# A 4-layer hybrid decoder step on one core: adaLN units placed elsewhere around the pooling layers and two hand-overs

## Chip, cores and metric

The kernel runs on one core of one Trainium2 chip. The metric is the device time of one execution in microseconds, here the median of several runs.

## What is computed

One inference step of a decoder trunk of four layers, with the same weights for a prompt of 256 tokens and for 8 samples of 4 tokens each. D_MODEL is 1024, D_FF 2816. Cut to what matters:

```python
for i in range(DEPTH):                       # 4 layers
    kind, j = i % 3, i // 3
    mod = (silu(c) @ w_ada[i] + b_ada[i])    # six vectors of 1024 for each sequence
    shift1, scale1, gate1, shift2, scale2, gate2 = mod
    h = rms_norm(x, norm_gain[i, 0]) * (1 + scale1) + shift1
    if kind == 0: mix, st = pool_mixer(h, pool_past[j], pos0, pool_w[j], pool_scale[j])
    elif kind == 1: mix, bufs = dilated_attention_mixer(h, ...)
    else: mix, st = gla_mixer(h, gla_past[j], ...)
    x = x + gate1 * mix
    h = rms_norm(x, norm_gain[i, 1]) * (1 + scale2) + shift2
    f, st = conv_ffn(h, conv_past[i], ffn_w_in[i], ffn_conv_w[i], ffn_conv_b[i], ffn_w_down[i])
    x = x + gate2 * f
y = rms_norm(x, final_gain)
```

Layers 0 and 3 pool, layer 1 is dilated attention, layer 2 is GLA (gated linear attention). A pooling layer also returns the samples' last 15 rows of pooling input, 11 of which are copied from the old state.

## The kernel before

All of x stays in SBUF, transposed (features on partitions), as `x` of 8 tiles of 128 features by 288 tokens (256 of the prompt, 32 of the samples). Weights come in units of 1 MB through six `raw` buffers, loaded by SyncE's queue. A product in full precision is made of three: a weight tile is split into a high part `whi` (ScalarE, line 345) and a low part `wlo` (VectorE, line 353), the activations into `hh` and `hl`, and TensorE adds hh*whi, hl*whi and hh*wlo (lines 414 to 416).

The adaLN vectors (`mod`) of a layer come from w_ada, 24 units of 1 MB. A *unit* here is one such load and its matmuls on the `adaps` tile in PSUM (line 534, four column tiles side by side, a moving operand of 512 columns). Units stand in groups; a group gives one or two of the six vectors. `adaps` has one buffer, so a group's end has two steps: its evacuation to `adasb` by ScalarE (line 544), and its finish, four transposes on TensorE (`ps<-adasb`, line 410) with VectorE's additions into `modT` and `modA` (lines 555 to 563). `modA` of a layer is what its norms multiply by.

The order of the program is written by hand as lists of step names: `POOL_ORDERS`, `ATTN_ORDER`, `GLA_ORDER`, `FFN_RUNS`. Every engine follows this order in its own queue. A `+` stands for the next unit of the queue of units, whatever it is. In the first layer the units of groups 1 to 3 are named: b10 to b13 are the units of the first of them, b14 its evacuation, b15 its finish, and likewise b20 to b25 and b30 to b35. In `fill` (line 218), the end of a group is put behind its last unit by three pieces of weights for the evacuation and five for the finish, and earlier in two cases: a step with `need` makes what it needs come out, and a unit that is the `first` of its group makes all pending ends come out ahead of it, since it writes `adaps` anew.

Between the mixer and the FFN of a layer, and between layers, lies a *hand-over*: two `+`, then the sums of squares over x on TensorE (`sqps`, line 596), then the norm. The norm is a chain: ScalarE takes the root (`ny`, `nv`, lines 635 and 636), VectorE makes `rstd` of it (lines 638 to 642), multiplies it with x and `modA` (`ht`, line 674), ScalarE adds the shift and rounds (`hh`, line 705) and VectorE takes the rest (`hl`, line 710). In the FFNs of layers 1 and 2 four `+` follow the norm in the order, and cover it on TensorE.

A pooling layer normalizes, multiplies by its weights in two products (`product0`, `product1`, lines 1019 to 1021), then does the samples' part. `dd` (the samples' differences, last made on GpSimd at line 1000) is multiplied in `ys0` and `ys1` (lines 1042 to 1045: matmuls with 64 or 32 moving columns), then `add0` and `add1` (lines 1056 to 1060) apply the pooling matrices to the prompt. `past` (line 959) prepares the old state ahead of the layer and, at its end, issues the copy of the 11 rows, a DMA from DRAM to DRAM on GpSimd's queue (line 975).

Of the kernel before, what the change touches and what calls it, by code (L numbers as in the profile page):

```python
# [41 lines left out]
norm b10 norm2 b11 product0 product1 ys0 b12 b13 b14 ys1 b15 gates b20 b22 b21 add0 squares0 b23 add1 b24 pre b30 squares1 b25 b31 root  # L42
early b32 b33 b34 b35 end
""", """
norm + + + + norm2 gates product0 product1 pre ys0 ys1 add0 squares0 add1 + + squares1 end
# [12 lines left out]
v0a z0 x2 v0b xc ms7 e2 v0c z1 m0a sb v0d sc ms5 m0b v1a x3 z2 m1a v1b e3 ms6 vv0 m1b + v1c x4 z3 m2a v1d e4 ks m2b +  # L58
v2a x5 z4 m3a v2b ps e5 vv1 m3b + v2c x6 z5 m4a v2d e6 up0 m4b + v3a kk0 z6 m5a v3b uo0 vv2 m5b + v3c ea m6a un0a v3d eb m6b un0b +
r0a ec m7a un0c up1 r0b vv3 m7b un0d kk1 gs0 + r0c cr uo1 r0d up2 un1a + r1a kr0 un1b r1b kr1 un1c op0 r1c un1d op1 kk2 gs1 r1d uo2 op2 up3  # L60
# [120 lines left out]
class Step:  # L181


    __slots__ = ("fn", "piece", "unit", "gap", "busy", "ahead", "key", "need", "first")
# [33 lines left out]
def fill(entries, queue):  # L218

    out, ends = [], []  # L220
    queue = list(queue)
    seen = 0

    def take():
        s = queue.pop(0)
        if s.first:
            while ends:
                out.append(ends.pop(0)[1])
        out.append(s)
        k = 3  # L230
        while queue and queue[0].busy:
            ends.append((seen + k, queue.pop(0)))
            k += 2
    for e in entries:
        if e == "+":
            if queue:
                take()
            continue
        if e.need is not None:
            while any(q.key <= e.need for q in queue):  # L240
                take()
            while any(q.key <= e.need for _, q in ends):
                out.append(ends.pop(0)[1])
        out.append(e)
        if e.piece is not None:
            seen += 1
            while ends and ends[0][0] <= seen:
                out.append(ends.pop(0)[1])
    if queue or ends:
        raise ValueError("units left")  # L250
    return out


class Trunk:
# [258 lines left out]
    def ada_steps(self, l, m0, nm, own=None):  # L513
# [53 lines left out]
        for k, s in enumerate(st):  # L567
            s.key, s.first = (l, m0), k == 0
# [356 lines left out]
    def pool_steps(self, l):  # L925
# [33 lines left out]
        def past(v):  # L959
# [15 lines left out]
            nc.gpsimd.dma_start(out=O["pool_s"][j, :, 0:11, :], in_=I["state_pool"][j, :, 4:15, :])  # L975
# [987 lines left out]
    def build(self):  # L1963
# [22 lines left out]
        for n, l in enumerate(Ls):  # L1986
            kind = l % 3
            after = None
            if kind == 0:
# [10 lines left out]
                after = p.pop("outs2")  # L2000
# [7 lines left out]
            if after:  # L2008
                f.insert(4, after)
# [12 lines left out]
            elif n:  # L2022
                f = ["+", "+", Step(lambda: self.sums()), f[0]] + list("+" * 4) + f[1:]
# [102 lines left out]
```

## Time and profile before

| | |
|---|---|
| median of 3 runs | 1376.65 us (1375.03 to 1380.5) |
| the profiled execution: its time, its span | 1377.05 us, 1375.3 us |
| mean granted clock of TensorE | 0.983 |
| busy: PE, PEld, DVE, ACT, POOL | 1324.9, 1196.7, 853.6, 639.2, 203.4 us |
| adaLN units: matmuls of line 534 on `raw` tiles | 736 records, 93.9 us busy |
| read from HBM, written | 300.21 MB, 19.76 MB |

PE is TensorE's matmuls, PEld its weight loads, DVE VectorE, ACT ScalarE, POOL GpSimd, SP SyncE. Times in rows are microseconds from the start of the span. In a timeline a row has its start, its length, engine, line, operation, the tile written and the tile read, a count, and in brackets how long the engine was idle before it and whose end released it. In windows of time the columns are the busy time of each engine, then the granted clock of TensorE (1.00 is full), the share of the DMA engines' time and GB/s. The trace counts two matmul records where the program has one matmul on 32-bit floats, so a unit is four matmuls in the program and eight in the trace.

### The profile page before, as it was taken

What the parts mean: (1) busy time and instruction counts of PE and PEld (TensorE: products, weight loads), DVE (VectorE), ACT (ScalarE), POOL (GpSimd) and SP (SyncE); (2) the same over time, 40 slices, a digit from 0 to 9 for tenths busy, and PEclk for the clock granted to TensorE, in tenths of its full rate; (3) what the DMA queues carried; (4) which work ended last, traced back from release to release, by engine and by line L of the source; (5) the groups of instructions that cost most, each with busy time, mean ns of one, the idle gap of its engine ahead of it and who ended that gap; (6) DMA issues with size and microseconds to landing.
All of it is one profiled execution on the core that took longest, in us unless ns stands there. A gap on an engine that the chain in (4) does not pass through costs nothing.

```text
span 1375.3 us, 25416 instructions
## 1 busy us (share of the span) xinstructions
PE 1324.9 (96%) x10075; PEld 1196.7 (87%) x10075; DVE 853.6 (62%) x1674; ACT 639.2 (46%) x1154; POOL 203.4 (15%) x492
## 2 busy tenths in 40 slices
PE   5899999999999999999999999999999999999997
PEld 3578899998886798899979887799999977999997
DVE  3576565556445776665566656687765566767654
ACT  3364444435444554444345344465444345555442
POOL 2220001002001112211024522121100022110100
PEclk8899999999999999999999999999999988999999
DMA  9998888559545787995494675885555566454520
GB/s 350 366 317 305 271 297 291 176 175 304 178 156 194 252 274 263 389 342 199 147 306 150 219 259 179 308 252 185 178 153 172 174 248 220 154 184 147 175 85 35
DMA packets 206231, 310.48 MB, mean 226 GB/s; under 512 B 7692, under 2 KB 186742, under 8 KB 196496
## 3 DMA queue, kind: packets, MB, share of 16 engines
q1 hardware_dynamic: 201296, 286.82, 62.4%
q0 software_dynamic: 4352, 21.50, 4.1%
q8 instruction: 79, 1.29, 0.4%
q10 hardware_dynamic: 464, 0.54, 0.1%
q14 instruction: 40, 0.33, 0.1%
HBM read 300.21 MB, written 19.76 MB: 233 GB/s over the span
## 4 chain that ended last, share of the span: by engine, by line
PE 84%; DVE 7%; ACT 3%; DMA 3%; POOL 1%; issue 1%; SPq 0%; DVEq 0%; POOLq 0%; ACTq 0%
PE mm L414 22%; PE mm L416 22%; PE mm L415 22%; PE adaps L534 4%; DMA raw<-w_ada 3%; PE ps L410 2%; DVE hl L710 1%; DVE ht L674 1%; DVE wlo L353 1%; PE mm L796 1%; PE ps L1670 1%; PE sqps L596 1%; PE mm L797 1%; PE mm L798 1%; ACT whi L345 1%
## 5 line engine op out<-in xcount | busy, mean ns | idle before, releaser
L414 PE MATMUL mm<-hh,whi 128*128 128x288 f32 x1720 | 514.6, 299 | 5.9 <-ACT hh L705 4.7
L415 PE MATMUL mm<-hl,whi 128*128 128x288 f32 x1720 | 509.6, 296 | 2.4 <-DVE hl L710 2.3
L416 PE MATMUL mm<-hh,wlo 128*128 128x288 f32 x1720 | 509.0, 296 | 2.0 <-DVE wlo L353 2.0
L353 DVE TENSOR_TENSOR wlo<-raw,whi 128x1024 fp32r<-128x1024 f32 (+2 forms) x335 | 398.7, 1207 | 140.0 <-ACT whi L345 139.7
L345 ACT ACTIVATE whi<-raw 128x1024 fp32r<-128x1024 f32 (+2 forms) x335 | 343.2, 1030 | 283.3 <-PE mm L415 204.7
L414 PEld LDWEIGHTS mm<-hh,whi 128*128 128x128 f32 x1720 | 323.4, 188 | 23.4 <-issue 11.5
L415 PEld LDWEIGHTS mm<-hl,whi 128*128 128x128 f32 x1720 | 323.6, 188 | 5.0 <-POOL hs L678 2.1
L416 PEld LDWEIGHTS mm<-hh,wlo 128*128 128x128 f32 x1720 | 323.4, 188 | 3.1 <-DVE wlo L353 2.7
L414 PE MATMUL mm<-ah,whi 128*128 128x288 f32 x704 | 208.5, 296 | 0.0
L416 PE MATMUL mm<-ah,wlo 128*128 128x288 f32 x704 | 208.0, 295 | 0.0
L415 PE MATMUL mm<-al,whi 128*128 128x288 f32 x704 | 206.9, 294 | 0.0
L415 PEld LDWEIGHTS mm<-al,whi 128*128 128x128 f32 x704 | 132.8, 189 | 0.0
L414 PEld LDWEIGHTS mm<-ah,whi 128*128 128x128 f32 x704 | 132.5, 188 | 0.0
L416 PEld LDWEIGHTS mm<-ah,wlo 128*128 128x128 f32 x704 | 132.3, 188 | 0.0
L853 DVE TENSOR_SCALAR c<-ext,vec 128x304 f32<-128x304 f32 x88 | 38.7, 440 | 120.2 <-ACT ext L850 117.8
L856 DVE SCALAR_TENSOR_TENSOR c<-ext,vec,c 128x304 f32<-128x304 f32 x176 | 94.9, 539 | 6.3
L534 PE MATMUL adaps<-raw,cT 128*32 128x512 f32 x736 | 93.9, 633 | 4.6 <-DMA raw<-w_ada 4.6
L862 POOL COPY convS<-ext 128x2 f32<-128x2 f32 x88 | 16.4, 186 | 458.8 <-ACT ext L849 458.8
L849 ACT ACTIVATE ext<-mm 128x256 f32<-128x256 f32 x88 | 34.0, 387 | 83.7 <-PE mm L416 83.7
L859 ACT ACTIVATE ge<-c 128x304 f32<-128x304 f32 x88 | 40.1, 460 | 57.6 <-DVE c L856 57.4
L872 DVE TENSOR_TENSOR a<-ge,mm 128x256 f32<-128x256 f32 x88 | 36.8, 418 | 43.9 <-PE mm L416 40.3
L534 PEld LDWEIGHTS adaps<-raw,cT 128*32 128x32 f32 x736 | 19.9, 112 | 48.6 <-issue 34.8
(394 smaller groups left out, 1497.6 us busy)
## 6 DMA issues: line engine op xcount, KB each, us to landing
raw<-w_ada SPq DMA_DIRECT2D x92, 1024.0 KB, 7.8
raw<-ffn_w_in SPq DMA_DIRECT2D x80, 1024.0 KB, 5.7
raw<-ffn_w_down SPq DMA_DIRECT2D x32, 1024.0 KB, 5.0
raw<-ffn_w_down SPq DMA_DIRECT2D x16, 768.0 KB, 4.2
raw<-gla_w_in SPq DMA_DIRECT2D x12, 1024.0 KB, 6.4
raw<-ffn_w_in SPq DMA_DIRECT2D x16, 512.0 KB, 5.3
win_s<-cache_win_g POOLq DMA_DIRECT2D x16, 512.0 KB, 7.1
raw<-attn_w_in SPq DMA_DIRECT2D x7, 1024.0 KB, 13.0
```

The costliest lines, as they stand in the source:

```text
L345: self.nc.scalar.activation(out=hv, in_=r, func=AF.Copy)
L353: self.nc.vector.tensor_tensor(out=lv, in0=r, in1=hv.bitcast(F32), op=ALU.subtract)
L410: self.nc.tensor.transpose(out=out, in_=in_, identity=self.ident[0:k, 0:k])
L414: mmul(out=out, lhsT=wh, rhs=xh, start=start, stop=False)
L415: mmul(out=out, lhsT=wh, rhs=xl, start=False, stop=False)
L416: mmul(out=out, lhsT=wl, rhs=xh, start=False, stop=stop)
L534: nc.tensor.matmul(out=ps[32 * q:32 * q + 32, :], lhsT=self.cT[:, k * per + r, :], rhs=v[:, r, j * 512:(j + 1) * 512], start=(k == 0), sto ...
L849: nc.scalar.activation(out=e[:, 2:258], in_=ps[t][:, 0:TP], func=AF.Copy)
L853: nc.vector.tensor_scalar(out=c1, in0=e[:, 0:304], scalar1=w[0], scalar2=self.vcol("ffn_conv_b", l * 22 + f), op0=ALU.mult, op1=ALU.add)
L856: nc.vector.scalar_tensor_tensor(out=c1, in0=e[:, k:k + 304], scalar=w[k], in1=c1, op0=ALU.mult, op1=ALU.add)
L859: nc.scalar.activation(out=ge, in_=c1, func=AF.Gelu)
L872: nc.vector.tensor_tensor(out=a[:, 0:TP], in0=ge[:, 0:TP], in1=ps[t][:, 0:TP], op=ALU.mult)
```

## The change

Four edits of the order; no arithmetic is changed.

1. First layer: b12 moves between `product0` and `product1`, b13 and the evacuation b14 move ahead of `ys0`, b20 ahead of the finish b15, b22 ahead of `gates`.
2. The copy of the 11 rows leaves `past` and becomes a step of its own, put at place 30 of the FFN of the same layer.
3. Two `+` leave the GLA layer, and two are put into the last pooling layer between `product1` and `ys0`.
4. `fill` no longer puts all pending ends ahead of the first unit of a group, only as far as the last evacuation among them; a finish then comes by its count of pieces or by a `need`. A new mark `E`, used in the FFNs of layers 1 and 2, puts a pending evacuation there, ahead of the sums.

```diff
-norm b10 norm2 b11 product0 product1 ys0 b12 b13 b14 ys1 b15 gates b20 b22 b21 add0 squares0 b23 add1 b24 pre b30 squares1 b25 b31 root
+norm b10 norm2 b11 product0 b12 product1 b13 b14 ys0 b20 b15 ys1 b22 gates b21 add0 squares0 b23 add1 b24 pre b30 squares1 b25 b31 root
-norm + + + + norm2 gates product0 product1 pre ys0 ys1 add0 squares0 add1 + + squares1 end
+norm + + + + norm2 gates product0 product1 + + pre ys0 ys1 add0 squares0 add1 + + squares1 end
-v0a z0 x2 v0b xc ms7 e2 v0c z1 m0a sb v0d sc ms5 m0b v1a x3 z2 m1a v1b e3 ms6 vv0 m1b + v1c x4 z3 m2a v1d e4 ks m2b +
+v0a z0 x2 v0b xc ms7 e2 v0c z1 m0a sb v0d sc ms5 m0b v1a x3 z2 m1a v1b e3 ms6 vv0 m1b v1c x4 z3 m2a v1d e4 ks m2b +
-r0a ec m7a un0c up1 r0b vv3 m7b un0d kk1 gs0 + r0c cr uo1 r0d up2 un1a + r1a kr0 un1b r1b kr1 un1c op0 r1c un1d op1 kk2 gs1 r1d uo2 op2 up3
+r0a ec m7a un0c up1 r0b vv3 m7b un0d kk1 gs0 r0c cr uo1 r0d up2 un1a + r1a kr0 un1b r1b kr1 un1c op0 r1c un1d op1 kk2 gs1 r1d uo2 op2 up3
...
         if s.first:
-            while ends:
+            while any(q.evac for _, q in ends):
                 out.append(ends.pop(0)[1])
...
+        if e == "E":
+            if ends and ends[0][1].evac:
+                out.append(ends.pop(0)[1])
+            continue
...
-            s.key, s.first = (l, m0), k == 0
+            s.key, s.first, s.evac = (l, m0), k == 0, k == NF // per
...
-            nc.gpsimd.dma_start(out=O["pool_s"][j, :, 0:11, :], in_=I["state_pool"][j, :, 4:15, :])
+        st["copy"] = Step(lambda: nc.gpsimd.dma_start(out=O["pool_s"][j, :, 0:11, :], in_=I["state_pool"][j, :, 4:15, :]))
...
-                after = p.pop("outs2")
+                after = [p.pop("outs2"), p.pop("copy")]
...
-                f.insert(4, after)
+                f[4:4] = after[:1]
+                f[30:30] = after[1:]
...
-                f = ["+", "+", Step(lambda: self.sums()), f[0]] + list("+" * 4) + f[1:]
+                f = ["+", "+", "E", Step(lambda: self.sums()), f[0]] + list("+" * 4) + f[1:]
```

The changed file's lines are numbered four higher from line 243 on (534 becomes 538). TensorE's order in the first layer, from the end of `product1` (`mm<-whi,hl`, `mm<-wlo,hh`) on. Before:

```order
L1020 MATMUL mm<-whi,hl 128x256
L1021 MATMUL mm<-wlo,hh 128x256
L1043 MATMUL ys<-dd,whi 128x64
L1045 MATMUL ys<-dd,wlo 128x32
L1042 MATMUL ys<-dd,wlo 128x32
```

Now:

```order
L1024 MATMUL mm<-whi,hl 128x256
L1025 MATMUL mm<-wlo,hh 128x256
L538 MATMUL adaps<-raw,cT 32x512 x4
L1047 MATMUL ys<-dd,whi 128x64
L1049 MATMUL ys<-dd,wlo 128x32
L1046 MATMUL ys<-dd,wlo 128x32
```

One unit (b13) now stands between the product and the samples' product; another (b12) stands in the same way between the two products.

TensorE's order at the hand-over from GLA to its FFN: the last product of the mixer, the hand-over, the transposes of the convolution's state (`ps<-cm,raw`) and the first product of the FFN. Before:

```order
L416 MATMUL mm<-hh,wlo 128x288
L534 MATMUL adaps<-raw,cT 32x512 x8
L596 MATMUL sqps<-ssq,ones 128x288
L596 MATMUL sqps<-sq,ones 128x288
L534 MATMUL adaps<-raw,cT 32x512 x8
L410 MATMUL ps<-cm,adasb 128x128 x4
L534 MATMUL adaps<-raw,cT 32x512 x8
L410 MATMUL ps<-cm,raw 128x88 x4
L414 MATMUL mm<-hh,whi 128x288
```

Now:

```order
L420 MATMUL mm<-hh,wlo 128x288
L538 MATMUL adaps<-raw,cT 32x512 x8
L600 MATMUL sqps<-ssq,ones 128x288
L600 MATMUL sqps<-sq,ones 128x288
L538 MATMUL adaps<-raw,cT 32x512 x16
L414 MATMUL ps<-cm,raw 128x88 x4
L418 MATMUL mm<-hh,whi 128x288
```

The finish of a group (`ps<-cm,adasb`) has left the place between the units behind the sums; this finish and another of the mixer's last products now come in the FFN. On ScalarE the evacuation ahead of the norm's root is now that of the group whose last unit stands ahead of the sums; before, it was that of the group whose last unit stands behind them.

TensorE's order at the hand-over from the last pooling layer to the last FFN, from the end of `add1` (`mm<-cb,zl`) on. Before:

```order
L1060 MATMUL mm<-cb,zl 128x128
L410 MATMUL ps<-cm,adasb 128x128 x4
L534 MATMUL adaps<-raw,cT 32x512 x8
L596 MATMUL sqps<-ssq,ones 128x288
L596 MATMUL sqps<-sq,ones 128x288 x4
L534 MATMUL adaps<-raw,cT 32x512 x8
L410 MATMUL ps<-cm,raw 128x88 x4
L414 MATMUL mm<-hh,whi 128x288
```

Now:

```order
L1064 MATMUL mm<-cb,zl 128x128
L538 MATMUL adaps<-raw,cT 32x512 x8
L600 MATMUL sqps<-ssq,ones 128x288
L600 MATMUL sqps<-sq,ones 128x288 x4
L414 MATMUL ps<-cm,adasb 128x128 x4
L538 MATMUL adaps<-raw,cT 32x512 x8
L414 MATMUL ps<-cm,raw 128x88 x4
L418 MATMUL mm<-hh,whi 128x288
```

The finish of the group that holds scale2 and shift2 of the last layer has moved from ahead of the units and the sums to behind both. VectorE's order is the same there: `modT`, `modA` and the samples' product with `modA` stand ahead of the norm's root.

More of the change, by code (lines that the diff above doesn't have):

```diff
@@ L181 @@
 class Step:
-    __slots__ = ("fn", "piece", "unit", "gap", "busy", "ahead", "key", "need", "first")
+    __slots__ = ("fn", "piece", "unit", "gap", "busy", "ahead", "key", "need", "first", "evac")
     def __init__(self, fn, piece=None, unit=None, gap=0, busy=False, ahead=None, need=None):
```

## Prediction

> **What bounds the kernel now.** I read the page first, then the list of who waited for whom, then windows of time with the granted clock, then the timeline at the places that the change touches.
>
> ```profile
> span 1375.3 us, 25416 instructions
> PE 1324.9 (96%) x10075; PEld 1196.7 (87%) x10075; DVE 853.6 (62%) x1674; ACT 639.2 (46%) x1154; POOL 203.4 (15%) x492
> ...
> PE 84%; DVE 7%; ACT 3%; DMA 3%; POOL 1%; issue 1%; SPq 0%; DVEq 0%; POOLq 0%; ACTq 0%
> ```
>
> TensorE is busy for 1324.9 of 1375.3 us, and 84% of the chain that ended last is its own work. The number of its instructions does not change here, so only 50.4 us of idle time, and time at a low clock, can be won. The list of waits (total, times, longest) says where PE stood:
>
> ```profile
> PE mm L414 <- ACT hh L705: 4.7, 3, 1.9
> PE adaps L534 <- DMA raw<-w_ada: 4.6, 4, 2.1
> PE ys L1043 <- POOL dd L1000: 2.2, 2, 1.1
> PE ps L410 <- ACT adasb L544: 2.2, 3, 0.7
> ```
>
> These four kinds are the ones that the change is near: FFN starts that wait for the norm, adaLN units that wait for their weights, the two pooling layers' sample products, and the ends of adaLN groups. The windows add what the waits do not show (the first number behind the PE, PEld, DVE, ACT and POOL columns is PE's granted clock):
>
> ```profile
> core 0: us, PE busy (x) PEld busy (x) DVE busy (x) ACT busy (x) POOL busy (x), PEclk, DMA share, GB/s
> 27.40:44.40 17.00, 13.80 (x60) 5.35 (x60) 5.62 (x15) 3.62 (x6) 2.14 (x6) 0.50 1.03 406
> 44.40:56.10 11.70, 9.40 (x72) 8.01 (x71) 10.49 (x22) 5.76 (x13) 6.11 (x12) 1.00 0.97 388
> 56.10:73.00 16.90, 16.85 (x130) 10.38 (x130) 9.47 (x25) 6.84 (x16) 0.00 (x0) 1.00 0.88 327
> 891.00:894.40 3.40, 1.28 (x11) 0.91 (x8) 2.92 (x7) 1.12 (x4) 2.34 (x5) 0.99 1.09 356
> 894.40:897.80 3.40, 3.40 (x17) 3.40 (x16) 3.40 (x9) 2.22 (x5) 0.66 (x1) 0.50 1.09 348
> 1123.00:1126.50 3.50, 2.40 (x22) 2.19 (x20) 2.61 (x7) 3.02 (x6) 1.18 (x6) 1.00 0.64 205
> 1126.50:1143.50 17.00, 17.00 (x79) 13.69 (x80) 10.21 (x26) 4.93 (x12) 0.00 (x0) 0.50 0.23 69
> ```
>
> Three stretches ran at half clock: the start, 3.4 us behind the GLA hand-over, and 17.0 us in the last pooling layer. 17.0 is five times 3.4, so the clock seems to be set in steps of 3.4 us. PE is fully busy in the last two, so they cost half their length, 1.7 and 8.5 us. Each follows a step in which PE did little.
>
> The profiled execution took 1377.05 us, 1.75 us more than its span, and 0.4 us above the median of 1376.65. I sum against 1377.05. About 0.5%, or 6.9 us, is what a measurement of this kernel can tell from no change.
>
> **The row copy.** It leaves the start, where DMA is full (share 1.03 at 406 GB/s in the window 27.40 to 44.40).
>
> ```profile
> 27.41 0.59 POOL L975 DMA_DIRECT2D pool_s<-state_pool  x1
> 34.79 1.93 PE L534 MATMUL adaps<-raw,cT 128*32 128x512 f32 x8 [1.60 <-DMA raw<-w_ada]
> 37.30 1.94 PE L534 MATMUL adaps<-raw,cT 128*32 128x512 f32 x8 [0.58 <-DMA raw<-w_ada]
> ```
>
> In the list of DMA issues (size of one, us to landing) it is:
>
> ```profile
> pool_s<-state_pool POOLq DMA_DIRECT2D x1, 352.0 KB, 6.7
> ```
>
> The copy runs while PE waits for the last two units of the first group, on which the first norm depends. 352 KB at 406 GB/s is 0.9 us. Bounds: 0, if it only used gaps, and -1.8 if reading and writing both count. I take **-0.9**. In the first layer's FFN it is one POOL issue of 0.59 us ahead of a small copy for the convolution. POOL is 15% busy and covers it, and the transfer lies beside products that no wait for DMA in the list belongs to, so I charge nothing; without that cover it would cost its 0.9 us there. The second layer's copy moves from one FFN to the next: nothing.
>
> **First pooling layer.**
>
> ```profile
> 54.15 0.30 PE L1043 MATMUL ys<-dd,whi 128*128 128x64 f32 x1 [1.09 <-POOL dd L1000]
> 56.05 1.92 PE L534 MATMUL adaps<-raw,cT 128*32 128x512 f32 x16
> ```
>
> PE is idle for 11.70 - 9.40 = 2.3 us from 44.4 to 56.1: 1.09 for dd and 1.2 for hl in the products. Two units cost 1.92 us at 56.05. Now one of them (b12) stands between the two products and one (b13) behind them. b13 fills the wait for dd. b12 delays the second product, whose waits for hl it covers; I put that at 0.7 of the 1.2 us, since most of the rest falls in the first product, ahead of it. The sample product then ends at 56.05 - 1.09 - 0.7 + 1.92 = 56.2 with both units done, where that was 56.05 + 1.92 = 58.0: **-1.8**. Bounds: -1.1 (only the wait for dd is filled) to -1.92. Behind it PE is full (16.85 of 16.90 us), so the gain is kept as far as the next norm, which starts earlier by it. The units' weights come in the same order as before. The group's evacuation stands at the same place of ScalarE's queue.
>
> **GLA layer.** Two units leave it.
>
> ```profile
> 757.76 1.06 PE L534 MATMUL adaps<-raw,cT 128*32 128x512 f32 x8
> 801.55 1.06 PE L534 MATMUL adaps<-raw,cT 128*32 128x512 f32 x8
> ```
>
> Neither has idle time ahead of it, so each is some 1.0 us of PE time: **-1.9** for both. They may have covered VectorE work, which then shows as a wait: bound -0.9.
>
> **GLA to FFN.** Below is this hand-over, then the same one behind attention, which has four units and no group's end in it.
>
> ```profile
> 885.94 1.92 PE L534 MATMUL adaps<-raw,cT 128*32 128x512 f32 x16
> 887.93 0.60 ACT L544 ACTIVATE adasb<-adaps 128x512 f32<-128x512 f32 x1 [3.68 <-PE adaps L534]
> 888.42 0.50 ACT L635 ACTIVATE ny<-sqps,eps 128x288 f32<-128x288 f32 x1
> 888.58 0.66 PE L410 MATMUL ps<-cm,adasb 128*128 128x128 f32 x4 [0.72 <-ACT adasb L544]
> 893.14 0.40 PE L414 MATMUL mm<-hh,whi 128*128 128x288 f32 x1 [1.60 <-ACT hh L705]
> ```
>
> ```profile
> 468.56 3.64 PE L534 MATMUL adaps<-raw,cT 128*32 128x512 f32 x32
> 472.57 0.38 PE L414 MATMUL mm<-hh,whi 128*128 128x288 f32 x1
> 479.87 0.40 PE L414 MATMUL mm<-hh,whi 128*128 128x288 f32 x1 [0.41 <-ACT whi L345]
> 481.13 0.40 PE L416 MATMUL mm<-hh,wlo 128*128 128x288 f32 x1 [0.73 <-DVE wlo L353]
> ```
>
> The sums end at 885.94, but ScalarE cannot start the norm's root (ny) until 888.42: the group's evacuation stands ahead of it in its queue and waits for two more units. In the changed order the group that ends here had its last unit before the sums, so its evacuation runs beside them; the ends' transposes go into the FFN. Then the place is like the one behind attention: the first FFN product 472.57 - 468.56 = 4.0 us behind the sums, where it was 893.14 - 885.94 = 7.2. That is -3.2; the half clock behind it goes, -1.7; the two waits that come behind attention (0.41 and 0.73) appear here, +1.1; the 0.66 us of transposes are paid in the FFN, +0.7. Sum **-3.1**. Bounds: -1.6 (the weights' split is later than I think), -3.8.
>
> **Last pooling layer.** Two units stand ahead of its sample products.
>
> ```profile
> 1124.76 0.30 PE L1043 MATMUL ys<-dd,whi 128*128 128x64 f32 x1 [1.10 <-POOL dd L1000]
> 1130.08 0.56 PE L1056 MATMUL mm<-cb,zh 128*128 128x256 f32 x1
> ```
>
> They fill 1.10 us and cost 1.92: **+0.8**. The half clock began at 1126.5, in the midst of the sample products, whose small matmuls (64 and 32 columns) leave the array nearly empty. With the wait filled, the thin stretch is 3.4 us of these products at full clock instead of 4.5. A step of 3.4 us can still lie mostly on it, but then the drop comes at its end, some 1.7 us of work later, which is one step less at half clock: **-1.7**, with bounds 0 and -8.5.
>
> [...]
>
> **Last hand-over.** The end of the group now stands behind the sums.
>
> ```profile
> 1139.77 0.50 DVE L555 TENSOR_TENSOR modT<-ps,vec 128x36 f32<-128x36 f32 x4 [0.39 <-PE ps L410]
> 1140.64 0.42 DVE L667 TENSOR_TENSOR hs<-x,modA 128x256 f32<-128x256 f32 x1
> 1146.30 1.92 PE L534 MATMUL adaps<-raw,cT 128*32 128x512 f32 x16
> 1146.94 0.53 DVE L638 TENSOR_TENSOR ssq<-ny 128x32 f32<-128x32 f32 x2 [5.88 <-ACT ny L635]
> 1149.81 0.40 PE L414 MATMUL mm<-hh,whi 128*128 128x288 f32 x1 [1.13 <-ACT hh L705]
> ```
>
> VectorE's queue holds modT, modA and hs ahead of L638. They took 1140.64 + 0.42 - 1139.77 = 1.3 us from the transposes' end. These now end 0.66 us behind the sums, so L638 starts 2.0 us behind them instead of 0.64: the norm is 1.3 us later, and so is the wait at 1149.81. The transposes themselves fill 0.6 us that stood ahead of the sums. **+0.7**; bounds +0.2 and +2.4 (a step at half clock, 1.7, on top).
>
> **Sum:** -0.9 - 1.8 - 1.9 - 3.1 + 0.8 - 1.7 + 0.7 = -7.9. 1377.05 - 7.9 = 1369.15, and I say **1369.0**.
>
> **Rivals.** (a) The last pooling layer keeps its full clock: the rest of the 8.5 us goes too, 1369.0 - 6.8 = 1362.2. For it: dense units now stand right up to the thin stretch. Against: the stretch is still as long as a step. What decides is where a step falls. [...]
>
> (b) The filler was not free: PE waits in GLA for VectorE (-0.9 in place of -1.9), the first pooling layer gives -1.1, and the FFN behind GLA waits for its split weights (-1.6). That takes back 1.0 + 0.7 + 1.5 = 3.2, about 1372.5. For it: DVE is 62% busy and its split of weights ends waits at FFN starts. Against: those two waits are in my sum already.
>
> (c) Slower than before: the first pooling layer falls to half clock as the last one does. The thin sample products are there too, and the start comes from half clock. Price: five steps, 8.5 us, 1377.5; if it lasts over all of the work from 56.1 to 73.0, which then takes twice its 16.9 us, 1386. It decides if a step sees mostly ys. Against: units stand on both sides of each of the two sample products, and the trace kept 1.00 from 44.40 to 56.10 with a 1.09 us wait in it.
>
> **Chances.** Forecast 0.52 (1366 to 1372), (a) 0.22, (b) 0.18, (c) 0.08. The mark for faster is 1376.65 - 6.9 = 1369.8. Of the forecast 0.34 lies below it, with (a) 0.56. Same: 0.18 + 0.18 and 0.05 of (c), 0.41. Slower: 0.03, the long form of (c). The range of 1361 to 1374 reaches over (a) and (b) and leaves out (c) and the edges.
>
> **What would show it.** Right: ys in the first pooling layer without a wait; ny about 0.1 us behind the sums at the GLA hand-over, the first FFN product near 4 us, clock 1.00 behind it; the waits for w_ada at the start shorter by 0.9; a wait of more than 1.13 us at the last FFN's first product. Wrong: a drop in the first pooling layer, new waits in GLA at the two places that lost a unit, or 17 us at half clock in the last pooling layer as before (then about 1370.7).

## The result and the profile after

| | before | after |
|---|---|---|
| median in one comparison, 20 runs each | 1380.78 us | 1374.74 us |
| ratio after to before, 95% interval | | 0.9948 [0.9927, 0.9969] |
| the profiled execution: its time, its span | 1377.05, 1375.3 us | 1372.64, 1370.9 us |
| mean granted clock in it | 0.983 | 0.987 |

One run of after, of 4466.52 us, stands outside the ratio and all that follows. The change gains 0.52%. Before took 1380.78 us in these runs, 4.1 more than the 1376.65 from which the forecast starts; by the ratio, 1376.65 becomes 1376.65 x 0.9948 = 1369.5 us, and the forecast was 1369.0. The absolute median of 1374.74 is 0.7 us above the range, because before was slower in these runs too. The two profiled executions differ by 4.4 us only, and that is the first thing to explain.

The page of after has the same work and 3.2 us less busy time of TensorE, in a span 4.4 us shorter.

```profile
span 1370.9 us, 25414 instructions
PE 1321.7 (96%) x10075; PEld 1193.4 (87%) x10075; DVE 854.0 (62%) x1674; ACT 638.1 (47%) x1154; POOL 201.2 (15%) x492
...
PE 38%; DVE 3%; ACT 1%; issue 1%; POOL 0%; DVEq 0%; POOLq 0%; ACTq 0%
```

Busy time fell though no matmul left: two steps of 3.41 us fewer of it ran at half clock, by the windows. The last row is the chain that ended last; it is followed back only to 777.09 us, to a unit with a new wait that is told below, so its shares are those of the time from there on and not to be set beside before's 84%. In after's list of waits (total, times, longest, in us) the four kinds shown of before read so:

```profile
PE adaps L538 <- DMA raw<-w_ada: 3.9, 4, 2.3
PE mm L418 <- ACT hh L709: 3.7, 2, 1.9
PE ps L414 <- ACT adasb L548: 2.1, 3, 0.7
PE adaps L538 <- ACT adasb L548: 1.8, 1, 1.8
```

The wait for `dd` has left the top of the list, the third FFN wait for `hh` is gone, and a new one has come: a unit that waits 1.8 us for an evacuation. (The lines of after that are shown here have the numbers of before plus 4.) The windows show where the clock was low (PEclk is the first number behind the engines' columns):

```profile
core 0: us, PE busy (x) PEld busy (x) DVE busy (x) ACT busy (x) POOL busy (x), PEclk, DMA share, GB/s
28.70:42.40 13.70, 10.13 (x47) 3.00 (x50) 4.82 (x12) 2.60 (x3) 0.58 (x2) 0.50 1.03 408
42.40:54.10 11.70, 10.15 (x73) 6.55 (x66) 9.61 (x21) 6.32 (x15) 7.05 (x14) 1.00 1.03 409
893.00:896.40 3.40, 2.26 (x16) 1.79 (x14) 2.05 (x4) 3.40 (x6) 1.10 (x2) 1.00 1.09 348
1121.00:1124.42 3.42, 3.42 (x32) 3.07 (x28) 3.42 (x6) 2.74 (x5) 0.00 (x0) 1.00 1.01 372
1124.42:1138.08 13.66, 13.66 (x64) 10.57 (x64) 7.03 (x18) 3.55 (x9) 0.00 (x0) 0.50 0.42 133
```

Behind the GLA hand-over the clock stays full, and in the last pooling layer the half clock lasts 13.66 us, four steps of 3.41 where before had five. The step ahead of the drop, 1121.00 to 1124.42, is busy to the last tenth.

The timeline at the places that the change touches: the first pooling layer's sample products; the new wait in GLA; the sums of the GLA hand-over end at 883.76, where the four units begin, with the root and the first FFN product behind them; and two finishes in that FFN.

```profile
52.98 1.06 PE L538 MATMUL adaps<-raw,cT 128*32 128x512 f32 x8
53.97 0.30 PE L1047 MATMUL ys<-dd,whi 128*128 128x64 f32 x1
...
577.81 1.07 PE L538 MATMUL adaps<-raw,cT 128*32 128x512 f32 x8 [0.56 <-DMA raw<-w_ada]
...
774.55 0.37 ACT L812 ACTIVATE vt<-mm 32x256 f32<-32x256 f32 x1 [5.64 <-PE mm L806]
774.95 0.66 ACT L1784 ACTIVATE v<-mm 128x256 f32<-128x256 f32 x2
775.49 1.06 ACT L1661 ACTIVATE X<-X 128x1024 f32<-128x1024 f32 x1
776.44 0.60 ACT L548 ACTIVATE adasb<-adaps 128x512 f32<-128x512 f32 x1
777.09 1.06 PE L538 MATMUL adaps<-raw,cT 128*32 128x512 f32 x8 [1.80 <-ACT adasb L548]
...
883.76 3.64 PE L538 MATMUL adaps<-raw,cT 128*32 128x512 f32 x32
883.87 0.50 ACT L639 ACTIVATE ny<-sqps,eps 128x288 f32<-128x288 f32 x1 [0.54 <-PE sqps L600]
887.64 0.38 PE L418 MATMUL mm<-hh,whi 128*128 128x288 f32 x1
...
905.73 0.60 PE L414 MATMUL ps<-cm,adasb 128*128 128x128 f32 x4
907.01 0.66 PE L414 MATMUL ps<-cm,adasb 128*128 128x128 f32 x4 [0.69 <-ACT adasb L548]
...
1145.43 0.40 PE L418 MATMUL mm<-hh,whi 128*128 128x288 f32 x1 [1.80 <-ACT hh L709]
```

The sample products start without a wait. `ny` starts 0.11 us behind the sums (2.5 before) and the first FFN product 3.9 us behind them (7.2 before). Against that stand three new waits: 0.56, 1.80 and 0.69 us.

### The profile page after: what moved, and what is told of

Its sections match the earlier page's. It is cut to its first block, busy times and chain, and to the rows that moved or that the text cites. A ratio compares the mean times of both kernels' runs of the same rounds, so it can differ in the third digit from the quotient of the medians.

```text
span 1370.9 us, 25414 instructions
## 1 busy us (share of the span) xinstructions
PE 1321.7 (96%) x10075; PEld 1193.4 (87%) x10075; DVE 854.0 (62%) x1674; ACT 638.1 (47%) x1154; POOL 201.2 (15%) x492
```

## The two questions

The profiles differ by 4.4 us, the medians by 6. Each run comes with its span and its mean granted clock c, so a run can be cut in two: c x span is the time that the work would take at full clock, (1 - c) x span what the half clock costs if TensorE has work all the while and half clock doubles its time (in before, the `ys` matmuls of 32 columns at lines 1045 and 1042 start 0.11 us apart at full clock, 1124.89 and 1125.00, and 0.22 at half, 1126.88 and 1127.10). Over all runs for which the clock is listed, before against after:

| | runs | mean span | c x span | (1 - c) x span |
|---|---|---|---|---|
| before | 84 | 1380.2 | 1353.2 | 27.1 |
| after | 27 | 1372.5 | 1352.0 | 20.5 |
| difference | | -7.7 | -1.2 | -6.5 |

The cut is not exact, since it also counts half clock where TensorE has little or nothing to do. The two profiled executions show how much that is. The cut gives them +1.9 for c x span and -6.3 for the clock, where the marks in their timelines, further down, give -1.0 for the waits and -3.4 for two steps of clock. Of the 6.3, 1.7 lie at the start (17.06 us at half clock in before, 13.66 in after, both with TensorE idle for over 3 us) and 1.2 behind the last matmul (6.46 and 4.09 us, TensorE busy for 0.00 us of both). Within before's runs the span falls by 1.10 us for each 0.001 of clock and not by 1.38; by that, the clocks' difference of 0.0046 is worth 5.1 us, and 2.6 are left for the waits. Both ways put most of the gain on the clock, where the forecast had 4.5 us of waits and 3.4 of clock. With the pair beside them, this split is an estimate, good to 2 or 3 us.

So there are two questions: where the filled waits went, and which part of the change moved the clock. In the expectations below, A is the theory of the forecast (the sum of filled waits, place by place, with two steps of clock), B and later S say that the gain is in where the steps at half clock fall, C that gains are swallowed by the weights' transfers, D that the clock falls where TensorE is idle, E that a step only falls later, and T that a step saved is lost again at the next place.

## Experiments: one part at a time

**First pooling layer alone** (before, with edit 1).

```diff
-... product0 product1 ys0 b12 b13 b14 ys1 b15 gates b20 b22 b21 add0 ...
+... product0 b12 product1 b13 b14 ys0 b20 b15 ys1 b22 gates b21 add0 ...
```

> Before with the first pooling layer's new order alone. Theory A (the gain is the sum of filled waits, place by place): the wait for dd ahead of the sample products (1.09 us) goes and the group's end that waits for adasb, at 76.74 before, comes 1.3 us earlier; nothing else moves, so the last layer's products at 1115.54 come 1.1 to 1.3 us earlier, and the last norm's sum too if the half clock in the last pooling layer lasts as long as before. Theory B (the difference between the two kernels is mostly where the steps of the clock fall): the events up to 1115 move by less than 0.5 us and the end by 1.7 us or a multiple of it. Theory C (gains upstream are swallowed later by the weights' transfers): -1.3 at 76.74, but -0.5 or less at the wait for w_ada at 702.15. Time: A 0.999 of before, B anything between 0.995 and 1.005, C 1.000.

Measured: 1378.47 us against 1380.31, ratio 0.9993 [0.9966, 1.002]. In the profile the stretch from the first group's finish (39.95 in before) to the finish that ends the layer's groups (76.74 in before) is 1.33 us shorter, as in after. At the first product of the GLA layer (705.82 in before, 705.68 here) it is still there, once one more step at half clock, from 78.7 to 82.1 us (at most 1.7), is taken off: A for the wait, not C. In the time, the gain is lost in the spread of the runs.

**Row copy alone** (before, with edit 2).

```diff
-            nc.gpsimd.dma_start(out=O["pool_s"][j, :, 0:11, :], in_=I["state_pool"][j, :, 4:15, :])
+        st["copy"] = Step(lambda: nc.gpsimd.dma_start(out=O["pool_s"][j, :, 0:11, :], in_=I["state_pool"][j, :, 4:15, :]))
```

> Before with the row copy moved alone. Theory A: the end of the first group, at 39.95 before, comes 0.7 us earlier (the two waits for w_ada ahead of it are shorter by that), and this is kept to 1115.54; no new wait in the first FFN. C: the same at 39.95, but given back by 702.15. A rival of A for this part, that the copy used only gaps of the transfers: 0 at 39.95. Time: A 0.9995, not to be told from 1.

Measured: 1383.01 us, ratio 1.0021 [0.9991, 1.005]. The first group's finish comes at 38.86 us, 1.1 earlier than in before's profile, but the same mark lies between 38.86 and 40.97 over all fourteen profiles, so one pair cannot tell 0.7 from 0. The worth of this part stays open between 0 and 1. What this profile did show is worth more. It took 1388.68 us, and these are its windows in the first pooling layer, which has before's order:

```profile
53.00:55.65 2.65, 2.61 (x24) 2.15 (x28) 2.18 (x4) 1.13 (x3) 0.00 (x0) 1.00 0.75 298
55.65:65.89 10.24, 10.24 (x52) 5.28 (x48) 0.92 (x5) 0.87 (x2) 0.00 (x0) 0.50 0.67 215
65.89:82.96 17.07, 14.82 (x114) 8.71 (x106) 13.60 (x39) 7.61 (x18) 1.33 (x6) 1.00 1.02 330
82.96:89.78 6.82, 6.12 (x24) 5.83 (x25) 5.14 (x11) 5.46 (x12) 2.20 (x4) 0.50 1.08 362
```

Three steps at half clock with TensorE fully busy, then two more at the FFN's start. So the first pooling layer of before does fall to half clock in some executions; the one that was profiled for the prediction was not among them.

**Two units alone** (before, with edit 3).

```diff
-... vv0 m1b + v1c ...  kk1 gs0 + r0c ...        gates product0 product1 pre ys0 ys1
+... vv0 m1b v1c ...    kk1 gs0 r0c ...          gates product0 product1 + + pre ys0 ys1
```

> Before with two units moved from the GLA layer to the last pooling layer, and the groups' ends where the old rule puts them. Theory A: in GLA the two units' 1.9 us are nearly all given back, since the first unit of the next group now forces the evacuation, which stands behind another step in ScalarE's queue (a wait of 1.8 us or more on adasb near 779): net 0 to -0.9 at the GLA norm's sum. At the GLA to FFN hand-over the evacuation no longer stands between the sums and ny: the first FFN product is near 5 us behind the sums instead of 7.2, and the half clock of 3.4 us there goes, together -2.5 to -3.2. In the last pooling layer the 1.10 us wait for dd goes, the half clock lasts 13.7 instead of 17.1 us (-1.7) and the units cost +0.8. Sum -3.5 to -4.8. Rival (it was the new rule for the ends that freed the hand-over): the hand-over stays at 7.2 us here, sum 0 to -2.

Measured: 1381.75 us, ratio 1.0004 [0.9974, 1.0034]. The wait of 1.80 us for `adasb` in GLA is there (at 791.52 in this profile), and a step at half clock came with it (791.47 to 794.88). No step fell behind the GLA hand-over, and four instead of five in the last pooling layer. The hand-over itself, with the lines numbered as in before and the sums ending at 899.76:

```profile
899.76 0.60 PE L410 MATMUL ps<-cm,adasb 128*128 128x128 f32 x4
899.96 0.50 ACT L635 ACTIVATE ny<-sqps,eps 128x288 f32<-128x288 f32 x1 [0.54 <-PE sqps L596]
904.28 0.40 PE L414 MATMUL mm<-hh,whi 128*128 128x288 f32 x1
```

`ny` starts 0.2 us behind the sums and the first FFN product 4.5 us behind them (2.5 and 7.2 in before). The hand-over is freed by the units, as A has it, not by the new rule. The sum expected, -3.5 to -4.8, does not show in the time.

**The rule for the ends alone** (before, with edit 4).

> Before with only the new rule for the groups' ends (a unit that begins a group forces the evacuation alone, and a mark for an evacuation). ScalarE's queue is then as before. Theory A: at the GLA to FFN hand-over ny is still behind the evacuation, 2.5 us behind the sums, and the first FFN product stays 7 us behind them; the transposes of two ends move into a product stretch (+0 to +0.7 each there, -0.7 each where they stood); the last hand-over's wait grows from 1.13 to 1.8 (+0.7, less the 0.6 of transposes that stood ahead of the sums). Sum -0.7 to +1. Rival (the rule frees the hand-over): first FFN product near 4 us behind the sums, sum -3.

Measured: 1379.9 us, ratio 0.9994 [0.9963, 1.0024]. Its timeline at the GLA hand-over, where the sums end at 891.74 when the units begin:

```profile
891.74 1.92 PE L538 MATMUL adaps<-raw,cT 128*32 128x512 f32 x16
893.73 0.60 ACT L548 ACTIVATE adasb<-adaps 128x512 f32<-128x512 f32 x1 [3.69 <-PE adaps L538]
894.22 0.49 ACT L639 ACTIVATE ny<-sqps,eps 128x288 f32<-128x288 f32 x1
897.61 0.40 PE L418 MATMUL mm<-hh,whi 128*128 128x288 f32 x1 [0.86 <-ACT hh L709]
```

`ny` still waits behind the evacuation, 2.5 us behind the sums as A has it, and the FFN starts 5.9 us behind them (A: 7, the rival: 4). So the new rule takes 1.3 us out of the hand-over but does not free it: `modT` and `hs`, which VectorE worked through between `ny` and line 638 in before, no longer stand there (line 642, 638 in before, starts 0.53 us behind `ny` here and 1.86 in before); the removal of two units from GLA does, because the group then ends ahead of the sums.

No part alone moves the time by more than the runs can tell. The four ratios multiply to 1.001, give or take some 0.006, against 0.9948: that they do not add up is only just outside the noise.

## Experiments: the new waits and the thin stretch

**A unit between the sample products** (after).

```diff
-... gates product0 product1 + + pre ys0 ys1 add0 ...
+... gates product0 product1 + pre ys0 + ys1 add0 ...
```

> After, with the last pooling layer's two extra units set apart: one ahead of the two sample products, one between them. Theory A (the clock falls in a step of 3.4 us in which PE streams little, busy or not): the unit's long rows break the thin stretch, no step falls there, and the 13.65 us at half clock from 1124.42 go: -6.8 us in the profile from there on, the mean granted clock of the runs rises from 0.985 to about 0.990 and their mean span falls from 1372.3 to about 1366. Rival D (the clock falls where PE stands idle): nothing is idle there in after either, so a unit that is moved by one product changes nothing: four steps at half clock as in after, mean clock 0.985, time of after; if the 0.1 us of the wait for dd that are left count, a little slower. Rival E (a step falls a product later): the half clock starts later and is one to three steps shorter, -1.7 to -5.

Measured: 1374.78 us, ratio 0.9928 [0.9902, 0.9954]; mean clock 0.985, as after. The last pooling layer:

```profile
1128.70:1132.16 3.46, 3.46 (x34) 3.42 (x31) 2.33 (x5) 0.48 (x3) 0.00 (x0) 1.00 0.89 288
1132.16:1142.40 10.24, 10.24 (x47) 7.01 (x46) 5.49 (x15) 3.16 (x8) 0.00 (x0) 0.50 0.40 127
```

The step that now draws the drop holds `ys1` and the first pooling matrices (line 1060 on) and no unit; three steps follow at half clock. That is E in this execution; in the one profiled execution of all three, below, which has the same order here, no step fell. A's "no step falls there" did not come, and A's mean clock of 0.990 neither. D falls as well, by after's own window 1121.00:1124.42: busy 3.42 of 3.42 us, no wait, and the clock drops at its end.

**The finish ahead of the last sums** (after; F puts all pending ends at its place).

```diff
-... add0 squares0 add1 + + squares1 end
+... add0 squares0 add1 F + + squares1 end
```

> After, with the end of the group at the last hand-over (four transposes and VectorE's modT and modA) put ahead of the units and sums of squares there, as it stands in before. If the 1.80 us wait at the last FFN's first product comes from VectorE's queue, where modT, modA and hs stand ahead of the norm, the wait falls by 0.5 (to 1.2 or 1.3; before has 1.13) and the end comes 0.5 us earlier than by the rest of after. If it comes from the sums alone: no change, or +0.1. Not to be told in the time of the runs, only in the profile.

Measured: 1373.33 us, ratio 0.9928 [0.9896, 0.9959]. Its timeline at the last hand-over, sums ending at 1140.74:

```profile
1138.51 0.42 DVE L671 TENSOR_TENSOR hs<-x,modA 128x256 f32<-128x256 f32 x1
1141.39 0.53 DVE L642 TENSOR_TENSOR ssq<-ny 128x32 f32<-128x32 f32 x2 [2.45 <-ACT ny L639]
1144.25 0.40 PE L418 MATMUL mm<-hh,whi 128*128 128x288 f32 x1 [1.13 <-ACT hh L709]
```

`hs` is done long before the sums, VectorE waits for `ny` and not for its own queue, and the wait is 1.13 us where after has 1.80. The queue was the cause of these 0.67 us. The hand-over as a whole wins less. From the last matmul of `add1` to the FFN's first product, with time at half clock counted half, it takes 8.82 us in before, 9.49 in after and 9.28 here (8.87 in the kernel with two waits out, below), since the transposes stand ahead of the sums again: 0.2 to 0.6 us. Its last pooling layer, with the same code as after up to there, had no step at half clock at all:

```profile
1125.99:1129.40 3.41, 3.41 (x35) 2.57 (x27) 3.41 (x5) 3.30 (x6) 0.33 (x5) 1.00 0.92 348
1129.40:1143.00 13.60, 13.44 (x102) 8.97 (x101) 9.97 (x32) 5.21 (x13) 0.38 (x1) 1.00 0.81 262
```

Here a step began 0.9 us ahead of `ys0`, in a unit; in after it began 0.35 us ahead. The steps' grid stood differently to the work in the two executions, and with the same code up to there they had 0 and 13.7 us at half clock.

**The evacuation in GLA one product earlier** (after; E puts a pending evacuation at its place).

```diff
-v2a x5 z4 m3a v2b ps e5 vv1 m3b + v2c x6 z5 m4a v2d e6 up0 m4b + ...
+v2a x5 z4 m3a v2b ps e5 vv1 m3b + v2c E x6 z5 m4a v2d e6 up0 m4b + ...
```

> After, with the evacuation of the group that ends in the GLA layer put into ScalarE's queue one product earlier, ahead of the steps that wait for later products. If the 1.80 us wait for adasb at 777.09 is there because the evacuation is forced by the next group's first unit, behind X in ScalarE's queue, it goes (0 to 0.3 left), and the sums behind GLA come 1.5 to 1.8 us earlier by the rest of after. If the wait only moves to another step of the chain through X (a product of the level that waits for ScalarE or VectorE), less than 0.5 is won. In the mean over the runs: -1.5, or -3 where the wait had drawn a step at half clock now and then; by the rival 0.

Measured: 1370.29 us, ratio 0.9903 [0.9866, 0.9939]. In its timeline the evacuation stands ahead of `vt`, `v` and X in ScalarE's queue and the unit has no wait:

```profile
771.33 0.60 ACT L548 ACTIVATE adasb<-adaps 128x512 f32<-128x512 f32 x1 [0.76 <-PE adaps L538]
...
776.88 1.07 PE L538 MATMUL adaps<-raw,cT 128*32 128x512 f32 x8
777.15 1.06 ACT L1661 ACTIVATE X<-X 128x1024 f32<-128x1024 f32 x1
```

In before, with its two units in place, the evacuation also stood ahead of `vt` and `v` (778.01 there), and the next group's unit had no wait:

```profile
769.58 0.60 ACT L544 ACTIVATE adasb<-adaps 128x512 f32<-128x512 f32 x1
772.01 1.06 PE L534 MATMUL adaps<-raw,cT 128*32 128x512 f32 x8
```

From the first product of the GLA layer (705.82 in before, 705.93 here) to GLA's norm (line 1901 in before, 851.85 and 849.27) the layer is 2.7 us shorter than in before; after is 0.8 shorter. The wait did not move to another step: it was worth 1.85 us.

**All three.**

> After with all three: the unit between the sample products, the group's end ahead of the last sums, the evacuation in GLA one product earlier. Theory A: -6.8, -0.5 and -1.7 add up to -9, mean span near 1363.5, ratio to before 0.988 to 0.990, mean clock 0.990. Theory D: -2 (1370), ratio 0.994.

Measured: 1370.83 us, ratio 0.9919 [0.9886, 0.9952]. Both waits are gone in its profile (GLA 2.7 us shorter than before, 1.13 us at the last FFN), and no step fell in its last pooling layer; but its mean clock is 0.986, hardly more than after's 0.985. The time is between A and D, and the unit between the sample products has no gain that the runs can tell.

## Experiments: after with one part undone

**Before's order in the first pooling layer** (after, edit 1 undone).

> After, with the first pooling layer in the order of before. Over ten profiles so far, the old order had 0, 3, 3 and 1 steps at half clock from 55 to 68 us, the new order none in six. Theory S (the gain is in the places where the clock falls): the wait of 1.1 us for dd is back (+1.3) and with it a chance of one to three steps at half clock there (1.75 on average, 3.0 us), so the mean of the runs is 4 us above that of after, ratio to before 0.998. Theory A (only the waits count): +1.3, ratio 0.996. Theory T (the steps fall anywhere, and a step saved here is lost at the next hand-over, near 80): +1.3 or less.

Measured: 1379.35 us, ratio 0.9973 [0.994, 1.0005]. That is nearer to S (0.998) than to A (0.996), but the interval holds both. Its own profile is one of the better ones (span 1370.8, no step in the first pooling layer), but three of its 12 runs took over 1384 us.

**The two units back in GLA** (after, edit 3 undone).

> After, with the two units back in the GLA layer. Then the evacuation of the group that ends behind GLA stands between the sums and ny again, ny is 2.5 us behind the sums, the first FFN product 7 us; one step at half clock comes back there (+1.7), and the last pooling layer has five steps again, where after and the kernels made from it had 4, 4, 3 and 0 (2.75 on average, +3.8). In GLA the two units cost 1.9 and the wait of 1.8 for adasb at 777 goes (0). In the last pooling layer the units' 1.9 against the wait of 1.10 for dd is given back (-0.8). Theory S: 4 to 5 us above after, ratio 0.998. Theory A, by waits alone: -0.8 to 0 to after, ratio 0.994.

Measured: 1375.99 us, ratio 0.9957 [0.9936, 0.9977], between A (0.994) and S (0.998, just outside the interval), and not to be told from after in the same set (0.9951, below). `ny` is 2.5 us behind the sums again; in this execution no step at half clock came of it, and four in the last pooling layer.

**After again, beside them.**

> After, as it is, beside the two above on the same chip, so that they are compared with it there and not across chips. Ratio to before near 0.995. In its profile, by S, a step at half clock neither from 55 to 68 us nor behind the GLA hand-over, and zero to four in the last pooling layer, as the steps happen to lie.

Measured: 1374.44 us, ratio 0.9951 [0.9924, 0.9979]. The waits of 1.80, 0.69 and 1.80 us come again, and that for w_ada in the attention layer's FFN (0.47 us at 580.02). Four steps in the last pooling layer.

**After with both new waits taken out.**

> After, with the evacuation in GLA one product earlier and the group's end ahead of the last sums, without the unit between the sample products. Both waits were 1.8 us in after; they went to 0 and 1.13 when done one by one. By that, -1.85 and -0.67: 2.5 us under after, ratio to before near 0.993, faster than both kernels. If the mean over the runs is set by where the clock falls, and these waits draw no steps, no more than that.

Measured: 1370.57 us, ratio 0.9907 [0.9876, 0.9938]: faster than before, and 3.9 us below after in the same set, though the two ratios' intervals overlap. The three kernels with both or the larger wait out have c x span = 1349.7 over 19 runs, against after's 1352.0 over 27: -2.3, give or take 0.8. The 1.85 us of the one wait and the 0.2 to 0.6 of the last hand-over would give that.

**Steps at half clock** (3.41 us each) by place, one profile per kernel, from the granted clock in each trace. Left out are three to five steps at the start, and the end of the span, which is at half clock in every kernel:

| kernel | first pool, 53-70 us | FFN start, 77-92 | 159-174 | 374-385 | 434-454 | GLA, 780-795 | behind GLA | last pool | last FFN start |
|---|---|---|---|---|---|---|---|---|---|
| before | 0 | 0 | 0 | 0 | 1 | 0 | 1 | 5 | 0 |
| copy alone | 3 | 2 | 2 | 1 | 1 | 0 | 1 | 5 | 1 |
| ends alone | 1 | 2 | 0 | 1 | 1 | 0 | 1 | 4 | 1 |
| units alone | 3 | 2 | 2 | 1 | 1 | 1 | 0 | 4 | 0 |
| after, old first pool | 0 | 0 | 0 | 0 | 1 | 0 | 0 | 3 | 1 |
| first pool alone | 0 | 1 | 0 | 0 | 1 | 0 | 1 | 5 | 0 |
| after, units back | 0 | 2 | 1 | 0 | 1 | 0 | 0 | 4 | 0 |
| after | 0 | 0 | 0 | 0 | 1 | 0 | 0 | 4 | 0 |
| after again | 0 | 1 | 0 | 0 | 1 | 0 | 0 | 4 | 0 |
| after, ys split | 0 | 2 | 1 | 0 | 1 | 1 | 0 | 3 | 0 |
| after, finish first | 0 | 2 | 0 | 0 | 1 | 1 | 0 | 0 | 1 |
| after, evacuation early | 0 | 2 | 0 | 0 | 0 | 0 | 0 | 3 | 1 |
| after, two waits out | 0 | 2 | 2 | 1 | 1 | 0 | 0 | 3 | 0 |
| after, all three | 0 | 1 | 2 | 1 | 1 | 0 | 0 | 0 | 0 |

The first five have before's order in the first pooling layer. They alone have steps there, in three of five. The runs say the same with more weight: of the kernels with the old order 32 of 132 runs took over 1384 us (before itself 17 of 84), of those with the new order none of 94. Behind GLA a step fell in four of the five kernels with the two units in GLA and in none of the nine without. The last pooling layer had 4.6 steps on average with no unit ahead of `ys0` (before and the kernels with copy, ends and first pool alone, and units back), and 3.0 with two units ahead of it (seven kernels). The new wait in GLA drew a step at 780 to 795 in three of the six kernels that have it, and no kernel without it has one there.

In before's trace the edges in the record of the granted clock lie 115, 116, 249, 250, 317, 322 and 388 times 3.413 us behind the one at 44.44, in after's 115, 116, 317, 321 and 388 times behind the one at 42.40; with the units alone, 57.60 and 791.47 are 215 times 3.413 us apart. So the time from the last edge to the start of `ys0` can be read off, and it differs by chance from execution to execution:

| place and order | us from the last edge to `ys0`: steps at half clock |
|---|---|
| first pool, before's order (5 profiles) | 0.49: 3; 0.80: 3; 1.02: 1; 2.88: 0; 2.92: 0 |
| first pool, new order (9) | 0.25, 0.30, 0.58, 0.88, 1.06, 1.34, 1.46, 3.11, 3.30: 0 each |
| last pool, no unit ahead of `ys0` (5) | 0.77: 4; 1.26: 4; 1.48: 5; 1.70: 5; 1.98: 5 |
| last pool, two units ahead (7) | 0.31: 4; 0.34: 4; 0.82: 4; 0.91: 0; 1.85: 3; 2.50: 3; 3.28: 3 |

In the first pooling layer before's order falls at some places of the grid, and the new order does not at the same places: there the order is the cause, as the runs over 1384 us say too. In the last one the drop is shorter with the two units on average, and with the grid's place it lasted 4, 4, 4, 0, 3, 3 and 3 steps.

## Why the prediction was right, and where its steps were not

The time was right, the split was not. By the marks in the two profiles:

| term | forecast | before to after in the profiles |
|---|---|---|
| row copy | -0.9 | first finish 39.95 to 39.28: -0.7; not told from the spread |
| first pooling layer | -1.8 | 76.74 to 74.74: -1.3 of it |
| weights in the attention layer's FFN | 0 | the wait at 577.81: +0.5 |
| GLA, two units | -1.9 | 851.85 to 849.47: -0.8 of it |
| GLA to FFN, clock in it -1.7 | -3.1 | 1115.54 to 1111.45: -1.7 of it |
| last pooling layer and last hand-over, clock in it -1.7 | -0.2 | 1149.81 to 1145.43: -0.3 of it |
| sum | -7.9 | -4.4 (1366.17 to 1361.76, where the last sums start) |

- *First pooling layer.* The wait for `dd` went as said; b12 covered 0.2 us of the waits for `hl`, not 0.7 (with the first pooling layer alone, three of before's four waits in the two products, 0.45, 0.28 and 0.22 us, are still there, and only the last, 0.23, is gone). The term is 1.3: in all nine profiles with the new order the stretch between the finishes at 39.95 and 76.74 is 1.32 to 1.34 us shorter than in before.
- *GLA.* "Neither has idle time ahead of it" was true, and the two units did leave 1.9 us. The step that failed is the look at what else they set: taking out one `+` moves the group's end on by one place. The next group's first unit then forces the evacuation, and this now stands behind `vt`, `v` and X in ScalarE's queue, which wait for TensorE's products: 1.80 us at 777.09. "New waits in GLA at the two places that lost a unit" was named as a sign of error; the wait came at a third place. With the evacuation earlier, GLA gains 2.7.
- *GLA to FFN.* `ny`, the first product, the full clock and the two waits (0.41 and 0.72, forecast 0.41 and 0.73) came as worked out. The transposes were mis-sized: two finishes now stand together in the FFN, and the second waits for the one `adasb`: 0.60 + 0.69 + 0.66 = 1.95 us where 0.7 was put. What the hand-over won without the clock, 1.4 by the forecast, is 0 between the two profiles: -1.7 in all, and one step of clock is 1.7.
- *Rival (b)*, that the filler was not free, thus came true in GLA (-0.8, it had -0.9), for another reason than a wait for VectorE.
- *Last pooling layer.* One step less at half clock, no wait ahead of `ys`, the last FFN's wait 1.80, the last hand-over 0.67 us longer (8.82 to 9.49): all as said in this profile. But rival (a), full clock there, happens too: in one execution of the seven with two units ahead of `ys0`, and in one of two with the units set apart. How little its small matmuls stream is seen in before's trace: at full clock those of 32 columns start 0.11 us apart (1124.89, 1125.00) and those of 256 columns 0.12 (1123.02, 1123.14).
- *Rival (c)* had the right place and the wrong sign. It feared that the change would make the first pooling layer fall to half clock. In fact before does so in some of its executions, and b12 and b13 end that. The forecast valued this part by one trace in which nothing fell.
- *The reading of before.* The prediction counts three stretches at half clock, each behind a step in which TensorE did little: for the start, which its rows do not show, TensorE was busy for 1.40 of 3.41 us (23.97 to 27.38). The trace has two more: a step at 436.98 us in the attention layer, which after has too (434.93), and the end of the span from 1368.81 on, where TensorE has no work. Neither is a term of the sum.

The profile pair has -1.0 for the waits (-4.4, less two steps of 1.7), and the runs have -1.2 to -2.6. So the forecast's 4.5 us of waits were too many by 2 to 3.5. The runs' total, -7.7 in mean span, still came out near the forecast's -7.9, because the clock won 5.1 to 6.5 by the runs and not 3.4. In the pair, where the clock won 3.4 by the marks, the total is -4.4. That the errors cancel in the runs is luck.

In the seven executions with two units ahead of `ys0`, a step's edge lies 0.31 to 3.28 us ahead of it. The drops differ in what stood ahead of them: before's clock fell at 1126.47 behind a wait of 1.10 us, with TensorE busy for 2.40 of 3.50 us (1123.00 to 1126.50); after's fell at 1124.42 behind 3.42 us in which TensorE was busy throughout by the profile, with matmuls of 64 and 32 columns.

**Open.** The first pooling layer alone gave 0.9993 [0.9966, 1.002], and its mean clock was before's, 0.981. Undone in after it cost 4.5 us of mean span against after in the same set, with a standard error of 2.3; the two units put back cost 1.5, with a standard error of 1.6. Neither is clear of 0. What is clear are the runs over 1384 us, which the new order in the first pooling layer ends: without them before's mean span is 1378.1 and not 1380.2, so they are 2.1 of the 7.7 us. For the rest, the table of steps has 0.8 of a step fewer behind GLA and 1.6 fewer in the last pooling layer, on average over the kernels, which would be 4.1 us of clock; the two units put back should undo both, and their 1.5 neither bears that out nor rules it out. It may be that each delay moves the work behind it on the grid, so that what one part saves another place can lose (the FFN start has steps in most kernels). No run has two parts together and the others not, and none set the grid's place, so this is argued and not shown.

## What to carry to other kernels

Look at more than one profiled execution where the clock falls in steps, and compare runs with their mean clock beside them: over 19 and 27 runs, clock x span told 2.3 us of waits, give or take 0.8, between kernels with nearly the same clock (0.986 and 0.985). Where the clocks differ more, it also counts half clock that costs nothing (in the pair 1.7 us at the start and 1.2 behind the last matmul). The first pooling layer's place with small matmuls was worth a filler though before's profile shows no drop there: up to 1.1 us of wait and then 1.9 of `ys0` drew a drop at three of five places of the grid, and 1.9 us of `ys0` between units at none of nine. By these counts, as an estimate, it is how much of one step such a place can fill by itself that matters. When a filler is moved, follow what its place sets besides its own time: here the place of a group's end decided behind which steps its evacuation stood in ScalarE's queue.

## What the runs showed of the hardware

- The clock fell at the end of a 3.42 us step with TensorE busy for all of it, in matmuls of 64 and 32 columns with some 0.35 us of a unit ahead (after, 1121.00 to 1124.42); it also fell with 0.82 us ahead (units alone, `ys0` at 1137.03), and did not fall at the end of a 3.41 us step with 0.91 us of a unit ahead of the same products (the finish ahead of the last sums, 1125.99 to 1129.40).
- Once down it stayed down for one to five steps (3.4 to 17.1 us), with TensorE fully busy in several of them: for 3.41 of 3.41 us (before, 436.98 to 440.39), 10.24 of 10.24 (copy alone, 55.65 to 65.89) and 17.07 of 17.07 (before, 1126.47 to 1143.54). In the last pooling layer the step at whose end it came back held 3.17 us of the 512-column units behind `add1` in before, 3.12 in after, 3.11 with the units back, 3.07 in after again and 1.4 with the old first pooling layer; the step ahead of that one held 0.47, 0.53, 0, 0.57 and 0 us of them.
- The steps lay on a grid of 3.413 us: 388 of them from 44.44 to 1368.81 in before, 388 from 42.40 to 1366.77 in after. The last edge ahead of the last pooling layer's `ys0` lies 1.70 us ahead of it in before, 0.34 in after and 0.31 in after again.
- One and the same kernel took 1374.6 to 1393.0 us (before, 84 runs, mean clock 0.972 to 0.989).
